# One-core transformer kernel: table loads two groups ahead, weights from block 46, 24 vector products in the first mixer, and new paces for the sparse rows

## The chip, the cores and the metric

The kernel runs as one program on one core of a Trainium2 chip. A core has five engines with an instruction queue each: TensorE (PE: matrix products; PEld is its loading of the stationary operand), VectorE (DVE), ScalarE (ACT), GpSimd (POOL) and SyncE (SP, which here issues nearly all transfers between the memory of the chip, HBM, and that of the core, SBUF). Each engine takes its instructions in order; an instruction that waits for a semaphore holds back all behind it on its engine. The metric is the device time of one execution in microseconds (us).

## The reference

The model is two blocks in a row on 512 tokens of width 1024. The first block mixes tokens (attention and a convolution), and then has a layer that picks 16 of 16,384 experts for each token and each of eight heads:

```python
def peer_ffn(h, lw):
    def chunk(xc):
        q = (xc @ wq).reshape(PEER_CHUNK, PEER_HEADS, 2, PEER_HALF)
        s = jnp.einsum('thpd,hpnd->thpn', q, keys)
        ...
        best_s, best_pos = lax.top_k(cand_s, PEER_TOPK)
        eid = jnp.take_along_axis(cand_i, best_pos, axis=-1)
        w = jax.nn.softmax(best_s.astype(jnp.float32), axis=-1).astype(xc.dtype)
        act = jax.nn.gelu(jnp.einsum('thkd,td->thk', jnp.take(u_tab, eid, axis=0), xc), approximate=False)
        return jnp.einsum('thk,thkd->td', w * act, jnp.take(v_tab, eid, axis=0))
```

Before each half of a block the activations are scaled and shifted by vectors that come from a conditioning vector: `silu(c) @ w_mod` in the first block and `silu(c_2) @ ada_w` in each layer of the second. The second block (two layers with a gated linear attention, a dense and a routed feed-forward layer) follows.

## The kernel before

**Float32 products.** TensorE multiplies in a shorter format, so each float32 operand is split into a high and a low part and each product is three matmuls (`mm3`, lines 153 to 155). `split` makes the parts of a weight tile of 128 x 1024: ScalarE copies the high part `wh` (L126), VectorE subtracts it for the low part `wl` (L128). `lin` is one product with a weight tile: 24 matmuls. `units` loads a weight tile into a buffer `raw` (L110) and splits it one ahead of its use. There are three buffers for `raw` in this part of the program, three for `wh` and three for `wl`.

**The expert layer** (`peer`) treats the tokens in two ways. For the first 384 (DN) it computes all 16,384 experts densely. For the last 128 it gathers the rows of the chosen experts.

- Dense, first table: 128 *blocks*, each one `lin` with a weight tile of `peer_u` for 384 tokens, a gelu on ScalarE (L1038), and a store of 192 KB to `Gd` in HBM (L1039).
- `choose`: top 16 of each head, and one-hot sums that turn positions into expert numbers, on VectorE, as background work that moves one step per block. `weigh` turns the choices for the dense tokens into a matrix of weights (one-hot products on VectorE, 16 small matmuls a block) and stores it to `Wd` in HBM, 2 MB for every four blocks. It begins with `turn`, which transposes the results of `choose` on TensorE (L971).
- Dense, second table: 30 *groups* (`values`) of four weight tiles of `peer_v`, 96 matmuls each, and then a 31st and 32nd. `weighted` prepares a group: it loads 768 KB of `Gd` and 768 KB of `Wd` into a buffer `gw` (L1061, L1062), multiplies them on GpSimd (L1066, four instructions), and splits the product into `cw` (L138, L139, four each).
- Sparse (`sparse`): 256 steps of one row per token each, 512 KB. GpSimd issues an indirect transfer for each row (L926), four to a buffer `rows`, one buffer ahead; VectorE multiplies a row of the first table with the tokens (L942) or adds a row of the second (L950). `pump` records so many steps per block or group.

The buffers `rows`, `gw`, `cw`, the tokens `h2h` and `h2l`, `own` and some more are *slabs*: all share one ring of 8 (`slab`).

**Vector products** (`gemv`): a modulation vector is made on VectorE, 128 elements an instruction, each with a weight tile of 512 KB (L330 loads it into a buffer `raw`, L331 multiplies and sums it). `over` spreads the conditioning vector first.

**What sets the order.** TensorE's order is that of the program. The instructions of the other engines, SP's and GpSimd's transfers among them, are put in order by a scheduler at build time, by priorities (background work has an offset: 300 for `sparse`, 100 for `choose`) and by when it reckons that they can run; buffers are given out in that order.

**Where the first mixer ends.** After attention there are three times eight products (`w_attn_o`, `w_conv_o`, `w_out`), of which 19 end with a tick of the background queues; each product uses one weight tile.

Of the kernel before, what the change touches and what calls it, by code (L numbers as in the profile page):

```python
# [11 lines left out]
F32 = mybir.dt.float32  # L12
F32R = mybir.dt.float32r
# [8 lines left out]
P = 128  # L22
# [10 lines left out]
DN = 384  # L33
# [362 lines left out]
    yield from gen  # L396


def mixer1(N):

    nc, I, sb = N.nc, N.I, N.sb
    V, A, PE, G = nc.vector, nc.scalar, nc.tensor, nc.gpsimd
    x = load_x(N)
# [9 lines left out]
    mods = sb.tile([P, 48], F32, name="mods")  # L413
# [47 lines left out]
    late = mod_multiplied(0)  # L461
# [17 lines left out]
    def gemv(f0, f1):  # L479
        return N.gemv(I["w_mod2"][f0 - 16:f1 - 16], f0, f1 - f0, lambda: cb, mods, N.v("b_mod"))  # L480
# [99 lines left out]
    for j in range(2):  # L580
        w = next(W)
# [20 lines left out]
    for h0, h1, slot in ((0, 2, 2), (2, 6, 4), (6, 8, 2)):  # L602
        ss = N.ps()
        items = []
        for h in range(h0, h1):
            pq = N.ps()
            N.lin(pq, next(W), hxh, hxl)
            i, at = slot + h - h0, 4 * (h - h0)
# [69 lines left out]
    for g in range(16):  # L678
        pg = N.ps()
        N.lin(pg, next(W), hxh, hxl)  # L680
        t = N.tmp([P, 512], name="gate")
# [39 lines left out]
    if norm:  # L721
        N.follow(delayed(delayed(norm)))
    N.lows = [V]
    N.background("gemv", gemv(24, 40), 1)
    Wa, Wc, Wo = N.units(I["w_attn_o"], 8), N.units(I["w_conv_o"], 8), N.units(I["w_out"], 8)
    ya = N.slab([P, 8, T], F32, "ya")
    for c in range(8):
# [25 lines left out]
        V.scalar_tensor_tensor(x[:, c, s], p, mods[:, 16 + c:17 + c], x[:, c, s], OP.mult, OP.add)  # L753
    last = ending(N, Wo, meh, mel, add)
    N.drain("gemv")
    return x, mods, gemv(40, 48), last


def peer(N, x, mods, last, gem=()):

    nc, I, sb = N.nc, N.I, N.sb
    V, A, PE, G = nc.vector, nc.scalar, nc.tensor, nc.gpsimd
# [238 lines left out]
    def weigh():  # L1001
# [6 lines left out]
        for q in range(DN // 8):  # L1008
# [16 lines left out]
                yield  # L1025
            o = nxt


    N.settle()
    for t in (DT, *range(DT)):  # L1030
# [3 lines left out]
    for i in range(NEXP):  # L1034
        p = N.ps()[:, :DN]
        N.lin(p, next(W), hh[:, :, :DN], hl[:, :, :DN])
        g = N.tmp([P, DN], name="gelu")
        A.activation(g, p, AF.Gelu)  # L1038
        nc.sync.dma_start(Gd[i], g)  # L1039
        if i == 9:  # L1040
            N.bg["choose"][1] = 1
            N.background("sparse", sparse(), 0, 300)
        if i == 62:
            N.drain("choose")
            N.background("pe_w", weigh(), 1)
        if i == 112:
            N.drain("pe_w")
            for e in gem:
                N.background("gemv", e, 1)
        if i > 9:  # L1050
            due += 1.2 if i < 62 else 1 if i < 112 else 1.2
            N.pump("sparse", int(due))
            due -= int(due)
    es.close()
    N.lows = [V]

    def weighted(g):

        x = N.slab([P, 2, 4, DN], F32, "gw")
        y = N.slab([P, 2, 4, DN], F32R, "cw")  # L1060
        nc.sync.dma_start(x[:, 0], Gd[4 * g:4 * g + 4].rearrange("i j t -> j i t"))  # L1061
        nc.sync.dma_start(x[:, 1].rearrange("p i t -> p (i t)"), Wd[g].rearrange("j c n -> j (c n)"))  # L1062
        w = x[:, 1].rearrange("p i t -> p (i t)").rearrange("p (c i t) -> p i c t", i=4, t=32)
        for i in range(4):
            ai = x[:, 0, i].rearrange("p (c t) -> p c t", t=32)
            G.tensor_mul(ai, ai, w[:, i])  # L1066
            N.cut(y[:, 0, i], y[:, 1, i], x[:, 0, i])
        return y

    def values(g, half, q, ps, y, s, first, last):  # L1070

# [8 lines left out]


    sums = [N.ps()[:, :DN] for _ in range(KT)]
    ahead = weighted(0)
    for g in range(30):
        y = ahead
        ahead = weighted(g + 1)
        for half in range(2):
            for _ in values(g // 2, half, g % 2, sums[4 * half:4 * half + 4], y, slice(0, DN), g == 0, g == 29):
                pass
            N.tick()  # L1090
            N.pump("sparse", 2)
    if "gemv" in N.bg:
        N.drain("gemv")
    N.drain("sparse")
    y = ahead, weighted(31)
    x = N.slab([P, KT, T], F32, "x")
    nc.sync.dma_start(x, xd)
    for k in range(KT):
# [1039 lines left out]
def build(tc, nc, I):  # L2138
    with ExitStack() as ctx:
        N = Net(ctx, tc, I)  # L2140
        N.setup()
        with tc.manual_schedule(engines={mybir.EngineType.PE}):
            with tc.tile_pool(name="early", bufs=1) as N.gp:
                N.gv = N.gp
                x, mods, late, last = mixer1(N)
                (m0, gem0), (m1, gem1) = (modulation(N, l) for l in range(2))
                x, last = peer(N, x, mods, last, (late, gem0(0, 16)))
                start = enter(N, x, last, m0)
            late = ExitStack()
            N.gp = N.late = late.enter_context(tc.tile_pool(name="late", bufs=1))  # L2150
            N.nraw = 6
            N.second()
            with tc.tile_pool(name="gemv", bufs=1) as N.gv:
                N.background("gemv", gem0(16, 48), 2)
                acc, last = mixer2(N, 0, x, *start, m0)
                start = next_input(N, x, acc, last, (0, 4, 7), N.v("ln1_g0"), N.v("ln1_b0"), m0[:, 32:40], m0[:, 24:32])
                N.background("gemv", gem1(0, 48), 1)
                x, acc, last = ffn(N, x, *start, m0)
                N.drain("gemv")
            start = next_input(N, x, acc, last, (0, 2, 3), N.v("ln2_g0"), N.v("ln2_b0"), m1[:, 8:16], m1[:, 0:8])  # L2160
            acc, last = mixer2(N, 1, x, *start, m1)
            late.close()
            N.gp = N.mp = ctx.enter_context(tc.tile_pool(name="moe", bufs=1))
            N.nraw = MOE_RAW
            moe(N, x, acc, last, m1)
# [11 lines left out]
```

## Time and profile before

| | |
|---|---|
| median of 3 runs | 3920.79 us (3920.43 to 3928.07) |
| the profiled execution | 3927.0 us, its span 3925.1 us |
| TensorE busy | 93% of the span |
| VectorE, ScalarE, GpSimd busy | 74%, 44%, 25% |
| transfers | 899 MB, 229 GB/s over the span |
| the 19 products that end the first mixer | 470.7 to 587.0 us |
| the 128 blocks, by their gelus | 769.8 to 1437.4 us |
| the 30 groups | 1444 to 2036 us |

The profile is one execution. A busy TensorE counts a matmul from its start to its modelled end, at either clock, so the granted clock has to be read beside it. The time of a stage is read from the starts of its gelus or matmuls, and what the stage waits for from the idle time of TensorE and of the engines that feed it.

### The profile page before, as it was taken

How to read it: one execution, taken by the hardware profiler on the slowest of the kernel's cores; microseconds unless marked ns; L12 is line 12 of the kernel's file. 1: busy time of each engine (PE TensorE's matmuls, PEld its weight loads, DVE VectorE, ACT ScalarE, POOL GpSimd, SP SyncE). 2: the span in 40 equal slices, each digit the busy share in tenths (PEclk: the TensorE clock that was granted, in tenths of full speed). 3: DMA queues.
4: the chain of work that ended last, by engine and by line, in shares of the span. 5: the costliest groups of instructions: out<-in, count | busy, mean ns of one | idle time of the engine just before them, and what ended most of it. 6: DMA issues, size and time to landing. Idle time of an engine off the chain costs nothing.

```text
span 3925.1 us, 61947 instructions
## 1 busy us (share of the span) xinstructions
PE 3646.8 (93%) x23129; PEld 3331.8 (85%) x23129; DVE 2897.0 (74%) x4938; ACT 1733.0 (44%) x2697; POOL 989.9 (25%) x936
## 2 busy tenths in 40 slices
PE   8999899987999778989999899999999999999996
PEld 5877778887999678889898788888889999999996
DVE  6799866999689766767855755554455788888898
ACT  3355543332444222323333223222324678787775
POOL 2212111054032344555523021002103304031211
PEclk9999999998999889999998999999998999999998
DMA  5322253389599988778864625663124799999997
GB/s 217 98 68 97 95 198 111 102 313 340 179 320 334 360 310 297 288 289 295 303 232 147 193 96 168 188 198 102 60 94 184 262 335 331 339 341 339 338 349 256
DMA packets 314758, 898.97 MB, mean 229 GB/s; under 512 B 28179, under 2 KB 114451, under 8 KB 312783
## 3 DMA queue, kind: packets, MB, share of 16 engines
q1 hardware_dynamic: 273583, 747.68, 55.7%
q0 software_dynamic: 40864, 147.25, 9.9%
q8 instruction: 183, 3.00, 0.3%
q14 instruction: 128, 1.05, 0.1%
HBM read 816.35 MB, written 78.46 MB: 228 GB/s over the span
## 4 chain that ended last, share of the span: by engine, by line
PE 39%; DMA 9%; DVE 6%; issue 5%; POOL 3%; ACT 2%; SPq 0%; DVEq 0%; POOLq 0%; ACTq 0%
PE ps L1819 10%; PE ps L154 9%; PE ps L155 9%; PE ps L153 9%; DMA gw<-Wd 3%; DVE wl L128 2%; DMA raw<-in_peer_v_dram 2%; ACT wh L126 1%; DMA rows<-in_peer_urows_dram,own 1%; DMA raw<-in_ada_w_dram 1%; DVE cw L139 1%; POOL gw L1066 1%; DMA rows<-in_peer_vrows_dram,own 1%; POOL mod L312 1%; DVE raw L331 1%
## 5 line engine op out<-in xcount | busy, mean ns | idle before, releaser
L126 ACT ACTIVATE wh<-raw 128x1024 fp32r<-128x1024 f32 (+1 forms) x1014 | 1050.2, 1042 | 1131.1 <-PE ps L154 594.9
L128 DVE TENSOR_TENSOR wl<-raw,wh 128x1024 fp32r<-128x1024 f32 (+1 forms) x1000 | 1221.5, 1235 | 310.9 <-ACT wh L126 295.0
L155 PE MATMUL ps<-h2h,wl 128*128 128x384 f32 (+2 forms) x1176 | 413.6, 352 | 46.1 <-DVE wl L128 46.1
L153 PE MATMUL ps<-h2h,wh 128*128 128x384 f32 (+2 forms) x1176 | 420.8, 358 | 32.1 <-ACT wh L126 27.7
L155 PE MATMUL ps<-cw,wl 128*128 128x384 f32 (+2 forms) x1088 | 376.0, 346 | 47.2 <-DVE wl L128 47.1
L154 PE MATMUL ps<-h2l,wh 128*128 128x384 f32 (+2 forms) x1176 | 410.2, 349 | 2.3 <-DVE h2l L139 2.1
L153 PE MATMUL ps<-cw,wh 128*128 128x384 f32 (+2 forms) x1088 | 372.5, 342 | 15.9 <-ACT wh L126 15.9
L154 PE MATMUL ps<-cw,wh 128*128 128x384 f32 (+2 forms) x1088 | 371.3, 341 | 0.0
L155 PEld LDWEIGHTS ps<-h2h,wl 128*128 128x128 f32 x1176 | 229.0, 195 | 59.9 <-DVE wl L128 55.1
L154 PE MATMUL ps<-ul,wh 128*128 128x512 f32 (+1 forms) x712 | 269.7, 379 | 8.5 <-DVE ul L139 7.8
L926 POOL DMA_INDIRECT rows<-in_peer_urows_dram,own x128 | 183.6, 1435 | 368.9 <-issue 203.4
L153 PE MATMUL ps<-uh,wh 128*128 128x512 f32 (+1 forms) x712 | 272.6, 383 | 3.4 <-ACT uh L138 2.3
L155 PE MATMUL ps<-uh,wl 128*128 128x512 f32 (+1 forms) x712 | 267.3, 375 | 0.0
L155 PEld LDWEIGHTS ps<-cw,wl 128*128 128x128 f32 x1088 | 215.7, 198 | 58.1 <-DVE wl L128 58.0
L153 PEld LDWEIGHTS ps<-h2h,wh 128*128 128x128 f32 x1176 | 229.6, 195 | 40.2 <-ACT wh L126 30.9
L331 DVE SCALAR_TENSOR_TENSOR raw<-raw,over 128x1024 f32<-128x1024 f32 x128 | 158.5, 1245 | 129.5 <-DMA raw<-in_ada_w_dram 105.3
L154 PEld LDWEIGHTS ps<-h2l,wh 128*128 128x128 f32 x1176 | 229.4, 195 | 7.8 <-DVE h2l L139 3.7
L926 POOL DMA_INDIRECT rows<-in_peer_vrows_dram,own x128 | 165.0, 1289 | 277.0 <-PE ps L971 88.1
L153 PEld LDWEIGHTS ps<-cw,wh 128*128 128x128 f32 x1088 | 215.7, 198 | 18.7 <-ACT wh L126 18.7
L950 DVE SCALAR_TENSOR_TENSOR own<-rows,own 128x1024 f32<-128x1024 f32 x127 | 171.0, 1346 | 74.3 <-DMA rows<-in_peer_vrows_dram,own 73.8
L942 DVE SCALAR_TENSOR_TENSOR rows<-rows,own 128x1024 f32<-128x1024 f32 x128 | 175.2, 1378 | 66.7 <-DMA rows<-in_peer_urows_dram,own 53.1
L1819 PE MATMUL ps<-xe,wh 128*128 128x352 f32 (+3 forms) x1408 | 221.9, 309 | 1.5 <-DVE xe L139 1.5
(529 smaller groups left out, 8579.7 us busy)
## 6 DMA issues: line engine op xcount, KB each, us to landing
raw<-in_moe_gu_dram SPq DMA_DIRECT2D x352, 512.0 KB, 5.8
raw<-in_moe_down_dram SPq DMA_DIRECT2D x160, 512.0 KB, 5.6
raw<-in_peer_v_dram SPq DMA_DIRECT2D x136, 512.0 KB, 6.2
raw<-in_peer_u_dram SPq DMA_DIRECT2D x128, 512.0 KB, 6.5
raw<-in_ada_w_dram SPq DMA_DIRECT2D x96, 512.0 KB, 4.4
raw<-in_w_in_dram SPq DMA_DIRECT2D x88, 512.0 KB, 3.9
Gd<-gelu SPq DMA_DIRECT2D x128, 192.0 KB, 5.4
Wd<-wst SPq DMA_DIRECT2D x12, 2048.0 KB, 14.1
```

The source lines that it names most:

```text
L126: self.nc.scalar.activation(h, src, AF.Copy)
L128: self.lows[-1].tensor_sub(l, src, f32(h))
L139: self.nc.vector.tensor_sub(l, src, f32(h))
L153: mm(out, ah, bh, start=start, stop=False)
L154: mm(out, ah, bl, start=False, stop=False)
L155: mm(out, al, bh, start=False, stop=stop)
L312: self.nc.gpsimd.tensor_scalar(t, x[:, k], sc[:, k:k + 1], sh[:, k:k + 1], OP.mult, OP.add)
L331: V.scalar_tensor_tensor(r, r, 1.0, b, OP.mult, OP.mult, accum_out=out[:, f:f + 1])
L926: G.indirect_dma_start(out=g[:, j], out_offset=None, in_=I[table], in_offset=bass.IndirectOffsetOnAxis(ap=oid[:, a:a + 1], axis=0))
L942: V.scalar_tensor_tensor(g[:, j], g[:, j], 1.0, ox, OP.mult, OP.mult, accum_out=oact[:, a:a + 1])
L950: V.scalar_tensor_tensor(oy, g[:, j], oact[:, a:a + 1], oy, OP.mult, OP.add)
L1819: PE.matmul(ps[j % 2][:, 0:n * (2 - i)], w[i][:, j * P:(j + 1) * P], rs[j // 2][i], start=first and i == 0 and j < 2, stop=last and i == p ...
```

## The change

- `weighted` is parted in two: `weights(g)` issues the two loads of group g, `weighted(x)` multiplies and splits. The loads of groups 0 and 1 are recorded at block 118, group 0 is made at block 125, and in the loop the loads run two groups ahead (before: one call made loads and products of the next group).
- `weigh` begins after block 46 (before 62), and what is left of `choose` is recorded at once there; `weigh` is drained at block 94 (before 112).
- Of the sparse rows 0.6 are recorded per block up to block 45, 1 up to 93, 1.6 up to 127 (before: 1.2 up to 61, 1 up to 111, 1.2 up to 127). Two per half group follow as before.
- The last 8 vector products of the first block's modulation and the first 16 of the second's (`gem0(0, 16)`), which were recorded from block 112 on, are recorded in the end of the first mixer, at two per tick; the 16 that were there already also go at two per tick.

```diff
@@ -396,7 +396,7 @@
     yield from gen
 
 
-def mixer1(N):
+def mixer1(N, gem):
 
     nc, I, sb = N.nc, N.I, N.sb
     V, A, PE, G = nc.vector, nc.scalar, nc.tensor, nc.gpsimd
@@ -721,7 +721,9 @@
     if norm:
         N.follow(delayed(delayed(norm)))
     N.lows = [V]
-    N.background("gemv", gemv(24, 40), 1)
+    N.background("gemv", gemv(24, 48), 2)
+    for e in gem:
+        N.background("gemv", e, 2)
     Wa, Wc, Wo = N.units(I["w_attn_o"], 8), N.units(I["w_conv_o"], 8), N.units(I["w_out"], 8)
     ya = N.slab([P, 8, T], F32, "ya")
     for c in range(8):
@@ -753,10 +755,10 @@
         V.scalar_tensor_tensor(x[:, c, s], p, mods[:, 16 + c:17 + c], x[:, c, s], OP.mult, OP.add)
     last = ending(N, Wo, meh, mel, add)
     N.drain("gemv")
-    return x, mods, gemv(40, 48), last
-
-
-def peer(N, x, mods, last, gem=()):
+    return x, mods, last
+
+
+def peer(N, x, mods, last):
 
     nc, I, sb = N.nc, N.I, N.sb
     V, A, PE, G = nc.vector, nc.scalar, nc.tensor, nc.gpsimd
@@ -1025,6 +1027,24 @@
                 yield
             o = nxt
 
+    def weights(g):
+
+        x = N.slab([P, 2, 4, DN], F32, "gw")
+        nc.sync.dma_start(x[:, 0], Gd[4 * g:4 * g + 4].rearrange("i j t -> j i t"))
+        nc.sync.dma_start(x[:, 1].rearrange("p i t -> p (i t)"), Wd[g].rearrange("j c n -> j (c n)"))
+        return x
+
+    def weighted(x):
+
+        y = N.slab([P, 2, 4, DN], F32R, "cw")
+        w = x[:, 1].rearrange("p i t -> p (i t)").rearrange("p (c i t) -> p i c t", i=4, t=32)
+        for i in range(4):
+            ai = x[:, 0, i].rearrange("p (c t) -> p c t", t=32)
+            G.tensor_mul(ai, ai, w[:, i])
+            N.cut(y[:, 0, i], y[:, 1, i], x[:, 0, i])
+        return y
+    loads = []
+
 
     N.settle()
     for t in (DT, *range(DT)):
@@ -1040,32 +1060,21 @@
         if i == 9:
             N.bg["choose"][1] = 1
             N.background("sparse", sparse(), 0, 300)
-        if i == 62:
+        if i == 46:
             N.drain("choose")
             N.background("pe_w", weigh(), 1)
-        if i == 112:
+        if i == 94:
             N.drain("pe_w")
-            for e in gem:
-                N.background("gemv", e, 1)
+        if i == 118:
+            loads += [weights(0), weights(1)]
+        if i == 125:
+            ahead = weighted(loads.pop(0))
         if i > 9:
-            due += 1.2 if i < 62 else 1 if i < 112 else 1.2
+            due += 0.6 if i < 46 else 1 if i < 94 else 1.6
             N.pump("sparse", int(due))
             due -= int(due)
     es.close()
     N.lows = [V]
-
-    def weighted(g):
-
-        x = N.slab([P, 2, 4, DN], F32, "gw")
-        y = N.slab([P, 2, 4, DN], F32R, "cw")
-        nc.sync.dma_start(x[:, 0], Gd[4 * g:4 * g + 4].rearrange("i j t -> j i t"))
-        nc.sync.dma_start(x[:, 1].rearrange("p i t -> p (i t)"), Wd[g].rearrange("j c n -> j (c n)"))
-        w = x[:, 1].rearrange("p i t -> p (i t)").rearrange("p (c i t) -> p i c t", i=4, t=32)
-        for i in range(4):
-            ai = x[:, 0, i].rearrange("p (c t) -> p c t", t=32)
-            G.tensor_mul(ai, ai, w[:, i])
-            N.cut(y[:, 0, i], y[:, 1, i], x[:, 0, i])
-        return y
 
     def values(g, half, q, ps, y, s, first, last):
 
@@ -1080,19 +1089,17 @@
 
 
     sums = [N.ps()[:, :DN] for _ in range(KT)]
-    ahead = weighted(0)
     for g in range(30):
         y = ahead
-        ahead = weighted(g + 1)
+        loads.append(weights(g + 2))
+        ahead = weighted(loads.pop(0))
         for half in range(2):
             for _ in values(g // 2, half, g % 2, sums[4 * half:4 * half + 4], y, slice(0, DN), g == 0, g == 29):
                 pass
             N.tick()
             N.pump("sparse", 2)
-    if "gemv" in N.bg:
-        N.drain("gemv")
     N.drain("sparse")
-    y = ahead, weighted(31)
+    y = ahead, weighted(loads.pop(0))
     x = N.slab([P, KT, T], F32, "x")
     nc.sync.dma_start(x, xd)
     for k in range(KT):
@@ -2142,9 +2149,9 @@
         with tc.manual_schedule(engines={mybir.EngineType.PE}):
             with tc.tile_pool(name="early", bufs=1) as N.gp:
                 N.gv = N.gp
-                x, mods, late, last = mixer1(N)
                 (m0, gem0), (m1, gem1) = (modulation(N, l) for l in range(2))
-                x, last = peer(N, x, mods, last, (late, gem0(0, 16)))
+                x, mods, last = mixer1(N, (gem0(0, 16),))
+                x, last = peer(N, x, mods, last)
                 start = enter(N, x, last, m0)
             late = ExitStack()
             N.gp = N.late = late.enter_context(tc.tile_pool(name="late", bufs=1))
```

**SP in the end of the first mixer** (L110 loads a weight tile of `w_conv_o`, L330 that of a vector product, both into one of the three `raw` buffers; the `sg` are gates). Before:

```order
L110 DMA raw_4377<-in_w_conv_o_dram 128x1024
L330 DMA raw_4407<-in_w_mod_dram 128x1024
L743 DMA sg_4497<-gates 128x512
L110 DMA raw_4418<-in_w_conv_o_dram 128x1024
L330 DMA raw_4448<-in_w_mod_dram 128x1024
L110 DMA raw_4460<-in_w_conv_o_dram 128x1024
```

After, at the same place:

```order
L110 DMA raw_4369<-in_w_conv_o_dram 128x1024
L745 DMA sg_4556<-gates 128x512
L330 DMA raw_4399<-in_w_mod_dram 128x1024
L330 DMA raw_4402<-in_w_mod_dram 128x1024
L110 DMA raw_4414<-in_w_conv_o_dram 128x1024
L330 DMA raw_4444<-in_w_mod_dram 128x1024
L330 DMA raw_4447<-in_w_mod_dram 128x1024
```

Per product the queue now holds three loads for the three buffers, where it held two.

**VectorE where `weigh` begins** (`wl` is the low part of a block's weights, L881/L883 the sums of `choose` into `pk`, L994 to L1000 the first one-hots of `weigh`). Before, the low parts of the 59th to the 66th block:

```order
L128 TENSOR_TENSOR wl_8729<-raw_8726,wh_8728 128x1024
L901 TENSOR_REDUCE z_8756<-pk_6184 128x8
L902 RECIPROCAL z_8756<-z_8756 128x8
L903 TENSOR_TENSOR pk_6184<-pk_6184,z_8756 128x128
L128 TENSOR_TENSOR wl_8770<-raw_8767,wh_8769 128x1024
...
L128 TENSOR_TENSOR wl_9018<-raw_9015,wh_9017 128x1024
L998 TENSOR_TENSOR oh_9004<-iota,wij_8971 128x1024
```

After, the low parts of the 50th and the 51st block and the 33 instructions between them, of which eight stand here:

```order
L128 TENSOR_TENSOR wl_8464<-raw_8461,wh_8463 128x1024
...
L888 TENSOR_TENSOR oh_8366<-kk_8125,steps 128x1024
L889 TENSOR_TENSOR oh_8367<-oh_8366,kk_8125 128x1024
L883 TENSOR_REDUCE pk_6275<-oh_8367 128x64
...
L981 TENSOR_TENSOR wij_8417<-ws_8422,wij_8417 128x768
...
L1000 TENSOR_TENSOR oh_8450<-iota,wij_8417 128x1024
...
L899 TENSOR_TENSOR oh_8378<-oh_8377,kk_8125 128x1024
L883 TENSOR_REDUCE pk_6275<-oh_8378 128x64
L996 TENSOR_TENSOR oh_8451<-iota,wij_8417 128x1024
...
L128 TENSOR_TENSOR wl_8528<-raw_8525,wh_8527 128x1024
```

Before, `choose` was through by the 59th low part, with seven low parts between it and the first one-hot of `weigh`. After, the last part of the choices stands right before `weigh`, in one piece. On TensorE `turn` stands in the middle of a block in both (after: of block 47, whose low part is the 48th).

**SP and VectorE among the groups.** SP, before and after, at the same group:

```order
L110 DMA raw_14014<-in_peer_v_dram 128x1024
L110 DMA raw_14044<-in_peer_v_dram 128x1024
L1061 DMA gw_14435<-Gd 128x4x384
L1062 DMA gw_14435<-Wd 128x1536
L110 DMA raw_14076<-in_peer_v_dram 128x1024
```

```order
L1033 DMA gw_14274<-Gd 128x4x384
L1034 DMA gw_14274<-Wd 128x1536
L110 DMA raw_14028<-in_peer_v_dram 128x1024
L110 DMA raw_14065<-in_peer_v_dram 128x1024
```

VectorE before, where `gw_14435` is cut:

```order
L128 TENSOR_TENSOR wl_14047<-raw_14044,wh_14046 128x1024
L139 TENSOR_TENSOR cw_14436<-gw_14435,cw_14436 128x384
L128 TENSOR_TENSOR wl_14079<-raw_14076,wh_14078 128x1024
L950 SCALAR_TENSOR_TENSOR own_6223<-rows_14428,own_6223 128x1024
L139 TENSOR_TENSOR cw_14436<-gw_14435,cw_14436 128x384 x3
```

and after, where `gw_14274` is cut:

```order
L128 TENSOR_TENSOR wl_14176<-raw_14173,wh_14175 128x1024
L952 SCALAR_TENSOR_TENSOR own_6314<-rows_14351,own_6314 128x1024
L139 TENSOR_TENSOR cw_14422<-gw_14274,cw_14422 128x384 x4
L128 TENSOR_TENSOR wl_14215<-raw_14212,wh_14214 128x1024
L952 SCALAR_TENSOR_TENSOR own_6314<-rows_14351,own_6314 128x1024
```

Before, the first cut of a group stood behind the low part of the weight tile whose load was issued just ahead of the group's own loads (`raw_14044`). After, four weight tiles and the loads of another group lie between: `raw_14173` is the fifth tile behind `gw_14274`.

## Rows read from the trace of the kernel before

**Rows 1.** The page's first part: span, then busy time, share, instructions.

```profile
span 3925.1 us, 61947 instructions
...
PE 3646.8 (93%) x23129; PEld 3331.8 (85%) x23129; DVE 2897.0 (74%) x4938; ACT 1733.0 (44%) x2697; POOL 989.9 (25%) x936
```

**Rows 2.** Busy time of engines by stretch, then granted clock, DMA share, GB/s.

```profile
470.70:587.00 116.30, 111.38 (x474) 88.10 (x473) 77.00 (x141) 54.34 (x73) 14.56 (x20) 0.99 0.54 179
862.00:963.00 101.00, 78.00 (x397) 74.03 (x396) 100.40 (x201) 28.63 (x43) 57.33 (x43) 0.90 0.93 358
1064.00:1316.00 252.00, 251.94 (x1933) 236.37 (x1930) 221.41 (x309) 117.57 (x194) 72.81 (x47) 1.00 0.99 322
1300.00:1350.00 50.00, 31.88 (x187) 29.42 (x185) 34.70 (x44) 9.85 (x18) 19.80 (x16) 0.83 1.05 386
1316.00:1444.00 128.00, 82.58 (x375) 76.64 (x375) 93.06 (x121) 34.39 (x61) 55.54 (x46) 0.81 0.95 344
1444.00:2036.00 592.00, 535.54 (x2880) 522.03 (x2881) 401.68 (x435) 177.14 (x243) 284.40 (x216) 0.95 0.79 288
2003.00:2036.00 33.00, 33.00 (x192) 33.00 (x191) 14.61 (x17) 8.39 (x8) 0.00 (x0) 1.00 0.60 208
```

**Rows 3.** Starts of the gelus, two stretches: times ns, first and last start us.

```profile
L1038 ACT ACTIVATE gelu<-ps x25: 469/490/492, 862.0 to 995.8; 128x384 f32<-128x384 f32 x25
...
L1038 ACT ACTIVATE gelu<-ps x14: 469/470/494, 995.8 to 1050.9; 128x384 f32<-128x384 f32 x14
```

**Rows 4.** Who waited for whom from 1444 to 2036 us: total us, times, longest.

```profile
POOL gw L1066 <- DMA gw<-Wd: 126.9, 17, 13.6
...
DVE own L950 <- DMA rows<-in_peer_vrows_dram,own: 70.6, 24, 6.8
...
DVE rows L942 <- DMA rows<-in_peer_urows_dram,own: 51.4, 22, 9.5
PE ps L155 <- DVE wl L128: 47.1, 30, 6.5
...
PE ps L153 <- ACT wh L126: 15.9, 9, 6.6
```

**Rows 5.** The costliest groups of instructions: busy us, mean ns, idle before.

```profile
L128 DVE TENSOR_TENSOR wl<-raw,wh 128x1024 fp32r<-128x1024 f32 (+1 forms) x1000 | 1221.5, 1235 | 310.9 <-ACT wh L126 295.0 <-PE ps L796 4.9
...
L126 ACT ACTIVATE wh<-raw 128x1024 fp32r<-128x1024 f32 (+1 forms) x1014 | 1050.2, 1042 | 1131.1 <-PE ps L154 594.9 <-issue 143.5 <-PE ps L155 98.5
...
L926 POOL DMA_INDIRECT rows<-in_peer_urows_dram,own x128 | 183.6, 1435 | 368.9 <-issue 203.4 <-DVE own L950 66.4 <-ACT wst L1022 31.3
L942 DVE SCALAR_TENSOR_TENSOR rows<-rows,own 128x1024 f32<-128x1024 f32 x128 | 175.2, 1378 | 66.7 <-DMA rows<-in_peer_urows_dram,own 53.1 <-issue 13.5
L950 DVE SCALAR_TENSOR_TENSOR own<-rows,own 128x1024 f32<-128x1024 f32 x127 | 171.0, 1346 | 74.3 <-DMA rows<-in_peer_vrows_dram,own 73.8
L1066 POOL TENSOR_TENSOR gw<-gw 128x384 f32<-128x384 f32 x128 | 167.7, 1342 | 196.9 <-DMA gw<-Wd 176.7 <-DMA raw<-in_w_mod_dram 8.6 <-PE ps L155 6.2
...
L331 DVE SCALAR_TENSOR_TENSOR raw<-raw,over 128x1024 f32<-128x1024 f32 x128 | 158.5, 1245 | 129.5 <-DMA raw<-in_ada_w_dram 105.3 <-DMA raw<-in_w_mod_dram 23.8
```

**Rows 6.** Transfers of the whole run: KB each, median us from issue to landing.

```profile
raw<-in_peer_v_dram SPq DMA_DIRECT2D x136, 512.0 KB, 6.2
...
gw<-Wd SPq DMA_DIRECT2D x32, 768.0 KB, 7.9
...
rows<-in_peer_urows_dram,own POOLq DMA_INDIRECT x128, 8.8
```

**Rows 7.** Loads into the `raw` buffers, issued from 483 to 558 us.

```profile
DMA to landing us min/median/max: 3.5/4.7/8.2
```

**Rows 8.** VectorE's groups of instructions from 770 to 963 us.

```profile
L881 DVE TENSOR_REDUCE pk<-oh 128x64 f32<-128x1024 f16 x18 | 21.6, 1212 | 0.0
...
L886 DVE TENSOR_TENSOR oh<-kk,steps 128x1024 f16<-128x1024 f16 x6 | 3.8, 681 | 0.0
```

**Rows 9.** SP's queue after the last store to `Wd`: start, us.

```profile
1322.50 20.31 SPq L330 DMA_DIRECT2D raw<-in_w_mod_dram  x1
```

## The prediction

> **What bounds the kernel now.** I read the first part of the page, then busy time by stretch. TensorE is busy for 93% of the span [rows 1], so a gain can only come from stretches in which it waits or runs at the lower clock. Rows 2 show three. From 862 to 963 us VectorE is busy 100.4 of 101 us and TensorE 78: VectorE bounds these blocks. From 1316 to 1444 us, the last 16 blocks, TensorE is busy 82.6 of 128 us at a granted clock of 0.81, and the DMA engines 0.95 of the time at 344 GB/s. From 1444 to 2036 us, the 30 groups, it takes 592 us, where the last two groups take 33.0 (192 matmuls without a gap at clock 1.00): 16.5 us a group, 495 for 30. So 97 us are lost there. From 1064 to 1316 us, by contrast, TensorE has no gap.
>
> What the groups lose their time to is in the waits [rows 4]: TensorE waits 47.1 us for low parts of weights and 15.9 for high parts, and the clock of 0.95 costs 5% of 535, some 27; together 90 of the 97. VectorE, which makes the low parts in order, stands 70.6 and 51.4 us for gathered rows, and GpSimd 126.9 us for `gw`. Why these go together: GpSimd issues the gathers and multiplies `gw` in one queue. While it waits for `gw` (7.9 us from issue to landing, rows 6), the next gathers are not issued; the rows come late; a low part stands behind a row on VectorE; TensorE waits for it. The order adds that the loads of `gw` stood one weight tile ahead of the cuts that need them.
>
> **The change part by part.** All terms are against the profiled execution, 3927.0 us (span 3925.1 and 1.9 around it).
>
> *The end of the first mixer: +20.* 24 vector products more: 24 x 1.245 = 30 us of VectorE [rows 5], which is busy 77 of 116.3 us there [rows 2], so its time alone is hidden. The buffers are not. Each product now needs three loads, and there are three. A buffer of a vector product is taken for landing 4.7 [rows 7], the product 1.3 and SP's issue 0.35: 6.4 us; that of a weight tile for 4.7, 1.04, 1.24 [rows 5] and 0.35: 7.3. The mean is 6.7 us a product, where the 19 took 116.3 / 19 = 6.1: +11. But 24 x 0.52 = 12.6 MB more raise 179 GB/s to some 287, at which the loads of the groups land after 6.2 [rows 2, 6]: then 8.2 us a product, +39. Three loads in flight hold 1.57 MB, which at 287 GB/s is 5.5 us; that gives 7.5 and +26. I take +20. Ends: 0 (landing 3.5 throughout, rows 7) and +45.
>
> *Blocks 24 to 48: -32.* 25 gelus lie 133.8 us apart, where 14 later ones lie 55.1 apart, 4.24 a block [rows 3]; at that pace 24 blocks take 101.8. The scheduler put 54 rows between these blocks' low parts before and 14 after: 40 x 1.36 = 54 us less for VectorE [rows 5], more than the 32 that it is late. Ends: -33 and -20.
>
> *The start of `weigh`: +23.* Here a new wait is added. `turn` stands in the middle of block 47 on TensorE and needs all choices. The low part of the 50th block can be made only when block 46 has given its buffer back, and the last choices stand behind it on VectorE. Up to the last sum they are 6 reductions of 1.212, 12 one-hot steps of 0.68 [rows 8], one step of 0.95, some 2 of small ones, and the low part of 1.24: 19.7 us, of which half a block (2.1) covers TensorE. 18 us are waited, and all later matmuls stand behind that. In the stretch with the long gaps the clock was 0.81 [rows 2]; 25 us at that clock lose 5. Ends: +10 and +30. Before, seven low parts lay between.
>
> *The other blocks: -2.* `weigh` takes 252 us as before; TensorE fills them [rows 2]. Blocks 48 to 63.5, which took 68 us at the pace of rows 3, and the 128 us of the last 16 blocks go; 32 blocks without `weigh` come. They carry 64 rows (33.5 MB), 32 weight tiles (16.8), 32 gelu stores (6.3), five groups' `gw` (7.9) and the last `Wd` (2.1): 66.6 MB. At the 344 GB/s of the last blocks before that is 194 us; TensorE needs 32 x 4.24 = 136. VectorE has 32 x 1.24 + 64 x 1.36 = 127. So the transfers bound it: 194 - 196 = -2. The scheduler put 56 of the 64 rows into the first 16 of these blocks, so little of it hides behind the rest. What went well before may go badly here too: behind the last store to `Wd` a load stood 20.3 us in SP's queue [rows 9]. Ends: -24 (172 us at 386 GB/s, the fastest of rows 2, which lasted 50 us) and +35 (231 us at 288).
>
> A page weighs on this term. HBM Reference of the Trainium skill (Specifications) has it that a core that streams alone, its neighbour idle, measures about 425 GB/s, and about 358 beside a streaming neighbour. No stretch here shows more than 386, and that for 50 us [rows 2]. By 425 the 66.6 MB would take an estimated 157 us and the term would be -39; by the row it is -2, and the row is taken.
>
> *The 30 groups: -69.* The loads of `gw` now stand five weight tiles ahead of the first cut, some 20 us, against 7.9 to land [rows 6] and 1.3 for the first product [rows 5]. So GpSimd no longer waits, and the gathers are issued as soon as their slab is free. What is late next: the weight tiles' own landing. I leave the 15.9 us behind high parts, a quarter of the 47.1, and no more than that of the clock: 495 + 28 = 523. The transfers allow it: 25 groups' `gw` (39 MB), 120 tiles (63) and 116 rows (61) are 163 MB, 312 GB/s over 523 us. Ends: -92 (500 us) and -26 (163 MB at 288 GB/s: 566).
>
> *After the groups: +3.* Ten rows more stand in the last two groups, 13 us on VectorE, which is busy 14.6 of 33 there [rows 2]; hidden but for a wait for a gather. Ends 0 and +13.
>
> Sum: 20 - 32 + 23 - 2 - 69 + 3 = -57. 3927 - 57 = 3870; the profiled execution is 6.2 above the median of the runs, so 3864.
>
> **The rivals.**
>
> *The transfers give no more than they gave the groups: slower.* If the 288 GB/s of the groups [rows 2] are what the DMA engines reach with gathers among the loads, and no result of late issue, the 32 blocks take 231 (+35) and the groups 566 (-26): 20 - 32 + 23 + 35 - 26 + 3 = +23, 3944. It decides below 297 GB/s, where 229.6 MB take the 774 us that would balance the sum. For it: a DMA share of 0.79 over the whole stretch. Against: 344 GB/s with the same mix just before.
>
> *Gathers stay the bound.* In the built program `gw` and `rows` share three slabs after the change, with one set of gathers in flight. A set takes four issues of 1.4, landing 8.8 and one row of 1.35: 15.8, and if GpSimd waits some 2.6 for the cut that frees the slab, 18.4 a group: 552 us, -40. The sum is then -28: 3893. For it: the waits for rows in rows 4. Against: the gathers alone are under 16.5.
>
> *All goes well.* Groups at 500, the 32 blocks at 172, the first mixer hidden: -32 + 23 - 24 - 92 + 3 = -122, 3799. Against: the DMA share of 0.95 in the last blocks [rows 2].
>
> *The first mixer eats it: no change.* With the slowest landing of rows 7, 8.2, a product takes 10.2 us: +78 in place of +20, sum +1, 3922. Against: it is the slowest, not the median.
>
> **How the numbers follow.** Forecast 47%, gathers 22%, all well 12%, transfers 12%, first mixer 7%. What is within 0.2% (8 us) can't be told from no change. Faster: nearly all of the forecast and of the gathers and the whole of the good case, 0.80. Same: most of the first mixer and a little of the gathers, 0.07. Slower: the transfers and one in a hundred of the rest, 0.13. The range takes in the good case at one end, 3800, and ends between no change and the transfers' rival at 3925; outside are most of the latter and half of the good case, under 2 in 10.
>
> **What would show it.** First mixer: the 19 products over some 136 us, with VectorE waiting for loads of L331's tiles. Blocks 24 to 48 at 4.24 us a gelu. A gap of TensorE of 18 us in block 47, released by VectorE's L883. The 32 blocks after `weigh` at some 6 us with 0.95 DMA share. The groups at 17.4 us, GpSimd's wait for `gw` near none, VectorE's for rows less than half. The prediction is wrong if the groups stay above 18.5 us, if the first mixer loses over 45 us, or if the gap in block 47 isn't there.

## Result and the profile after

The changed kernel takes 3954.86 us (median of 4 runs, 3952.0 to 3962.27), the kernel before on the same chip 3923.74: a ratio of 1.0083, 95% interval 1.0068 to 1.0098. It is slower by 31 us, where 57 us less were forecast. The profiled execution has a span of 3950.2 us, 25.1 more than before.

The page's first part of the kernel after; TensorE has the same work as in [rows 1].

```profile
span 3950.2 us, 61941 instructions
...
PE 3646.1 (92%) x23129; PEld 3328.6 (84%) x23129; DVE 2904.9 (74%) x4938; ACT 1735.7 (44%) x2697; POOL 1003.1 (25%) x936
```

Busy time by stretch of the kernel after: start:end, length, then the engines, granted clock, DMA share, GB/s. The stretches are the 19 products that end the first mixer (bounded as in [rows 2], where they took 116.3 us: from the first matmul to the issue of the last tile's load), blocks 24 to 46, `weigh`, the 32 blocks after it, the 30 groups.

```profile
478.20:615.60 137.40, 122.38 (x519) 95.12 (x518) 101.56 (x189) 56.32 (x77) 20.38 (x21) 0.96 0.68 228
890.00:986.00 96.00, 93.04 (x519) 92.72 (x518) 65.53 (x176) 35.12 (x48) 7.33 (x6) 0.98 0.63 222
1012.00:1264.00 252.00, 252.00 (x1917) 237.09 (x1915) 220.47 (x308) 119.68 (x196) 73.41 (x48) 1.00 0.97 322
1264.00:1472.00 208.00, 152.75 (x760) 145.26 (x758) 127.58 (x147) 52.82 (x86) 85.11 (x73) 0.87 0.82 303
1472.00:2064.00 592.00, 530.90 (x2879) 518.20 (x2879) 408.73 (x432) 178.31 (x251) 314.94 (x228) 0.96 0.78 289
```

The row to look at is the last: the groups, in which 69 us were to be won, take 592 us as in [rows 2], at the same rate, 289 GB/s for 288. VectorE's load from block 24 on, by contrast, fell as forecast (66 of 96 us busy, where it was 100 of 101).

Starts of the gelus after, two stretches (times in ns, first and last start in us):

```profile
L1058 ACT ACTIVATE gelu<-ps x23: 472/473/493, 887.7 to 986.4; 128x384 f32<-128x384 f32 x23
...
L1058 ACT ACTIVATE gelu<-ps x12: 472/472/491, 1011.5 to 1068.0; 128x384 f32<-128x384 f32 x12
```

The 23 lie 4.5 us apart, against 5.6 in the first row of [rows 3]. Between the two rows is the gap that `turn` makes: 25.1 us, for 4.2 at TensorE's pace. What TensorE waited for from 986 to 1012 us (total us, times, longest):

```profile
PE ps L973 <- DVE pk L883: 13.1, 2, 10.2
PE ps L973 <- DVE pk L905: 2.7, 1, 2.7
```

Who waited for whom in the groups after, from 1472 to 2064 us:

```profile
ACT wh L126 <- DMA raw<-in_peer_v_dram: 205.4, 51, 12.1
POOL gw L1043 <- DMA gw<-Wd: 111.1, 19, 10.4
DVE own L952 <- DMA rows<-in_peer_vrows_dram,own: 75.9, 32, 9.6
DVE rows L944 <- DMA rows<-in_peer_urows_dram,own: 74.9, 29, 7.9
...
POOL rows L928 <- DVE cw L139: 65.3, 17, 10.1
PE ps L155 <- DVE wl L128: 57.0, 32, 8.2
```

Two of these waits in the kernel before, from 1444 to 2036 us:

```profile
ACT wh L126 <- DMA raw<-in_peer_v_dram: 86.0, 30, 8.9
...
POOL rows L926 <- DVE cw L139: 44.7, 9, 7.8
```

GpSimd still waits 111 us for `gw` (126.9 in [rows 4]), VectorE more than before for rows (151 us for 122), TensorE 57.0 us for low parts (47.1). ScalarE waits 205 us for weight tiles (86.0 before). And GpSimd has a second wait in the same queue: before it can issue gathers it waits for a cut on VectorE, which frees the slab, 65.3 us for 44.7. The transfers of that stretch, median us to landing last (a tile took 6.7 in the groups before):

```profile
raw<-in_peer_v_dram SPq DMA_DIRECT2D x120, 512.0 KB, 9.3
...
gw<-Wd SPq DMA_DIRECT2D x27, 768.0 KB, 9.8
...
rows<-in_peer_urows_dram,own POOLq DMA_INDIRECT x56, 9.9
```

Why GpSimd still waits is in the chain of waits of the kernel after (start us, us, what):

```profile
1673.89 9.99 DMA gw<-Wd
...
1685.14 4.58 POOL gw L1043 x3
...
1690.87 1.72 POOL rows L928
...
1695.18 9.86 DMA rows<-in_peer_urows_dram,own
```

The load that is recorded two groups ahead is followed at once by its own multiplication, and the next gathers stand behind that. Pairing SP's `Wd` loads with the first multiplication and the last cut of the same group (groups 4 to 29, medians), the load is issued 9.3 us ahead of the multiplication before and 10.0 after; from there to the end of the cut it is 9.3 before and 27.9 after; and the finished product then lies 60 us before and 50 after until TensorE takes it. So the lead that was won lies behind the multiplication, where no one needs it.

### The profile page after: what moved, and what is told of

Same layout as the page of the kernel before. It is cut to its first block, busy times and chain, and to the rows that moved or that the text cites. A ratio compares the mean times of both kernels' runs of the same rounds, so it can differ in the third digit from the quotient of the medians.

```text
span 3950.2 us, 61941 instructions
## 1 busy us (share of the span) xinstructions
PE 3646.1 (92%) x23129; PEld 3328.6 (84%) x23129; DVE 2904.9 (74%) x4938; ACT 1735.7 (44%) x2697; POOL 1003.1 (25%) x936
## 4 chain that ended last, share of the span: by engine, by line
PE 43%; DMA 9%; DVE 6%; POOL 4%; issue 4%; ACT 1%; SPq 0%; DVEq 0%; POOLq 0%; ACTq 0%
PE ps L155 10%; PE ps L154 10%; PE ps L153 10%; PE ps L1826 10%; DMA rows<-in_peer_urows_dram,own 2%; DMA gw<-Wd 2%; DVE wl L128 2%; DMA rows<-in_peer_vrows_dram,own 1%; DMA raw<-in_peer_v_dram 1%; POOL gw L1043 1%; ACT wh L126 1%; POOL rows L928 1%; DVE rows L944 1%; DVE cw L139 1%; DMA raw<-in_moe_gu_dram 1%
## 5 line engine op out<-in xcount | busy, mean ns | idle before, releaser
L331 DVE SCALAR_TENSOR_TENSOR raw<-raw,over 128x1024 f32<-128x1024 f32 x128 | 156.5, 1230 | 93.7 <-DMA raw<-in_ada_w_dram 84.4
```

Of the source, the lines that this page charges most:

```text
L331: V.scalar_tensor_tensor(r, r, 1.0, b, OP.mult, OP.mult, accum_out=out[:, f:f + 1])
```

## The experiments

Theories for the groups. **Q**, the queue: the scheduler put the multiplication right behind its load, on GpSimd's one queue; gathers, rows, low parts follow late. **S**: the slabs that `gw` and rows share. **R**: the three buffers for weight tiles. **G**: one set of gathers in flight. **D**: the transfers give no more than 289 GB/s (the prediction's first rival). Ratios are to the kernel before on the same chip, with 95% intervals; "groups" is from the first matmul of group 0 to the last of group 29.

**e1_cw2.** Two fixed slabs for `cw`.

```diff
+        if len(cws) < 2:
+            cws.append(N.slab([P, 2, 4, DN], F32R, "cw"))
+        else:
+            cws.append(cws.pop(0))
+        y = cws[-1]
```

> The changed kernel, with the split products `cw` in two fixed slabs by turns, so that `gw` and `rows` share five slabs where the changed kernel left them three. The 30 groups took 592 us in the changed kernel, and 592 before. Theory S (the slabs: loads of `gw` and gathers wait for each other's buffers): the groups fall to 520 to 550 us, the kernel to 3885 to 3915, and GpSimd's wait for `gw` (111 us) goes below 40. Theory D (289 GB/s is what the transfers give with gathers among them): groups 585 to 600, kernel within 10 us of 3955. Theory R (three buffers for weight tiles, each held for its landing): groups 580 to 600 as well, and ScalarE's wait for tiles of `peer_v` (205 us) stays.

Measured: 3958.0 us, ratio 1.0078 (1.0057 to 1.0100); groups 597; GpSimd's wait for `gw` 120 us. S falls in this form: the room that came free only let GpSimd multiply earlier still (load to multiplication 9.0 us, multiplication to cut 69). The gathers' wait for a cut stayed, 66.6 us, so e1 doesn't say what that wait costs.

**e2_raw7.** Four more buffers, in turns with the three, during the groups.

```diff
+        if self.more:
+            self.turns += 1
+            if self.turns % 7 % 2 == 0:
+                return self.more.tile([P, 1024], F32, name=self.name("raw"), tag="rawx", bufs=4)
```

> The changed kernel, with seven buffers for the weight tiles of the 30 groups in place of three (in the room that the one-hot tiles leave). Theory R (the tile's landing, 9.3 us, in three buffers): groups at 530 to 560 us instead of 592, kernel 3890 to 3925, ScalarE's wait for tiles (205 us) below 60. Theory S (slabs): groups 580 to 595, since GpSimd's chain is not touched. Theory D (the transfers' rate): groups 585 to 600, landing of a tile longer than 9.3 us, rate still 285 to 293 GB/s.

Measured: 3924.5 us, 0.9991 (0.9981 to 1.0000); groups 565.5, at 298 GB/s. That lies just above the range of R (530 to 560) and below those of S and D: R is part of it (27 us), D is shaken.

**e3_cw2_raw7.** Both edits.

> Both edits at once: `cw` in two fixed slabs and seven buffers for weight tiles in the groups. Theory D: groups 580 to 600 us still, at 285 to 293 GB/s. Theories S and R: the groups at 500 to 530 us, 320 GB/s or more, kernel 3865 to 3895; if only one of the two is the bound, as that one alone.

Measured: 3924.7 us, 0.9986 (0.9973 to 0.9998); groups 562.4, as e2 alone. But the stretch has two parts (columns as above):

```profile
1468.00:1847.00 379.00, 335.00 (x1823) 327.39 (x1822) 257.17 (x268) 116.18 (x161) 203.36 (x148) 0.95 0.79 283
1847.00:2030.00 183.00, 183.00 (x1058) 183.00 (x1057) 162.25 (x163) 67.99 (x93) 98.76 (x80) 1.00 0.90 335
```

GpSimd's two waits in the second part:

```profile
POOL rows L933 <- DVE cw L144: 57.0, 9, 8.9
...
POOL gw L1052 <- DMA gw<-Wd: 2.6, 1, 2.6
```

The first 19 groups take 20.0 us each, the last 11 take 16.6, with all their loads and gathers, at 335 GB/s. That contradicts D. In these last groups the load lies 11 to 24 us (median 18) ahead of its multiplication, and of GpSimd's 80 us of waits for `gw` 2.6 fall here: this led to Q. The gathers' wait for a cut is long here, 57.0 us, and TensorE loses nothing by it (busy all of the 183 us).

**e4_half.** Gathered rows half as long in the groups.

```diff
-                G.indirect_dma_start(out=g[:, j], out_offset=None, in_=I[table],
+                G.indirect_dma_start(out=g[:, j, :512] if n >= 16 else g[:, j], out_offset=None,
+                                     in_=I[table].rearrange("n (b c) -> (n b) c", b=2) if n >= 16 else I[table],
```

> The changed kernel, with each gathered row half as long in the groups (2 KB in place of 4 KB for each of 128 tokens; half of each such row is left out of the result); the instructions, their order and their buffers stay. About 31 of the 171 MB of the groups go. Theory D (bytes at 289 GB/s): 140 MB take 484 us, so the groups come near TensorE's floor, 500 to 515 us instead of 592, and the kernel to 3870 to 3885. Theories S and R (chains of waits): the landings get shorter by a few us but the chains stay, groups 550 to 590, kernel 3915 to 3955.

Measured: 3895.8 us (one run); groups 535.8, at 261 GB/s, GpSimd's wait for `gw` 112 us. Between the two expectations: less to move shortens every landing (a gathered row 6.7 us for 9.9), but the rate falls well under 289, so it isn't a fixed rate that binds; it doesn't tell Q from R.

**e5_late.** The multiplication for group g+1 also waits for the first half of group g-1.

```diff
-            G.tensor_mul(ai, ai, w[:, i])
+            m = G.tensor_mul(ai, ai, w[:, i])
+            if mark:
+                N.tc.add_manual_dep(m.ins if hasattr(m, "ins") else m, mark, mybir.DependencyInfo(
+                    mybir.DependencyClass.Sync, mybir.DependencyReason.DATA), reason="late")
```

> The changed kernel, in which GpSimd's multiplication for group g+1 also waits for the first half of group g-1 on TensorE, so that it can't be put right behind its load. In the changed kernel 10.0 us (median) lie between the issue of a group's `Wd` load and its multiplication, 9.3 before, and the split products lie ready 50 us before their use. Theory Q (the lead of the loads was given away: the multiplication was moved up right behind the load, GpSimd stands for it and the gathers behind it): the distance rises above 18 us, GpSimd's wait for `gw` (111 us) falls below 30, the groups go from 592 to 525 to 560 us, the kernel to 3890 to 3925. Theory G (one set of gathers in flight, about 10 us of landing): the wait for `gw` goes, VectorE's waits for rows (151 us) stay above 120, groups 580 to 600, kernel 3940 to 3965. Theory R (three buffers for weight tiles, already shown to be worth 27 us of groups) as theory G.

Measured: 3924.7 us, 0.9992 (0.9980 to 1.0003); groups 555.9; load to multiplication 29.3 us. The waits of its groups:

```profile
POOL gw L1043 <- PE ps L153: 269.5, 29, 91.3
...
ACT wh L126 <- DMA raw<-in_peer_v_dram: 131.7, 33, 11.1
...
DVE own L952 <- DMA rows<-in_peer_vrows_dram,own: 50.1, 27, 5.2
DVE rows L944 <- DMA rows<-in_peer_urows_dram,own: 49.3, 28, 5.4
...
PE ps L155 <- DVE wl L128: 27.5, 18, 3.4
```

GpSimd waits for no `gw` load any more, and though it now waits much longer, for TensorE, rows come earlier (99 us of waits for 151) and TensorE's wait for low parts halves. The groups fit Q; the whole is at the edge of its range. The gathers still stand right behind the multiplication, but they no longer wait for a cut either (65.3 us without this edit, none here): the later multiplication takes away two waits at once, and the scheduler placed other work anew around it, so e5 shows what the edit is worth and not which wait made it so.

**e6_rows3.** Fixed slabs (made as in e1): three for rows with two sets in flight, two each for `gw` and `cw`.

```diff
+            while len(ahead) < (1 if N.fix is None else 2) and (job := next(more, None)):
+                ahead.append(gather(*job))
```

> The changed kernel, with fixed slabs in the groups: three for gathered rows and two sets of gathers in flight, two for `gw`, two for `cw`. Theory G: VectorE's waits for rows (151 us) fall below 60 and the groups to 530 to 560 us, kernel 3890 to 3925. Theory Q: GpSimd still stands over 80 us for `gw`, but that no longer reaches VectorE: also faster, groups 550 to 575. Theory R: rows' waits fall, TensorE then waits for weight tiles, groups 575 to 595, kernel 3935 to 3960.

Measured: 3959.4 us, 1.0074 (1.0057 to 1.0091); groups 606. All expectations of a gain miss: the scheduler issued all gathers in groups 0 to 8 (groups 3 to 8 took 32 us each), and left the rest without any. The first row below is groups 2 to 8, the second the others behind them.

```profile
1492.00:1709.00 217.00, 147.21 (x673) 138.13 (x672) 201.53 (x230) 43.09 (x69) 165.04 (x128) 0.82 0.98 377
1709.00:2065.00 356.00, 356.00 (x2017) 356.00 (x2016) 169.60 (x174) 129.56 (x169) 108.84 (x80) 1.00 0.63 210
```

It says little on G, but shows 377 GB/s over 217 us with gathers.

**e7_rows3_raw7.** e6 with the buffers of e2.

> The same fixed slabs with two sets of gathers in flight, and seven buffers for weight tiles in the groups. If late rows and the three buffers together are what holds the groups (G and R): 500 to 520 us, the pace at which twelve groups ran when both the slabs and the buffers were widened (16.7 us), kernel 3860 to 3885. If GpSimd's wait for `gw` is a bound of its own (Q): 550 to 570, as with seven buffers alone.

Measured: 3909.5 us, 0.9948 (0.9928 to 0.9967); groups 543.6. Between the two, and not to be read as either: the last gather is issued in group 15, so the last 12 groups, at 16.6 us, have no row left to gather, and the first 18, at 19, carry all of them. It says as little on G as e6.

**e8_late_raw7.** e5 and e2 together.

> The later multiplication and seven buffers for weight tiles. Q and R together: groups 505 to 530 us, kernel 3870 to 3895. R alone: 560 to 570 us, kernel 3920 to 3930. G: not below 560.

Measured: 3882.0 us, 0.9888 (0.9871 to 0.9904); groups 505.4. The groups, and two waits in them:

```profile
1453.00:1959.00 506.00, 502.35 (x2883) 500.93 (x2881) 403.06 (x430) 187.21 (x257) 348.25 (x241) 1.00 0.90 331
```

```profile
POOL gw L1048 <- PE ps L158: 172.1, 22, 85.3
...
PE ps L160 <- DVE wl L133: 3.6, 3, 2.8
```

TensorE is busy 502 of 506 us, with one set of gathers in flight as before, so G falls, and at 331 GB/s, so D falls. With e2 and e5 this is a full square of the two edits: 592, 566, 556, 505. Alone they bring 27 and 36, together 87: each alone leaves the other's wait in place.

**e9_before_late_raw7.** The same two edits in the kernel before.

> The kernel before, with the two edits that brought the changed kernel's groups to 505 us: the multiplication waits for the first half of group g-1 on TensorE, and seven buffers for weight tiles. The loads stay recorded one group ahead. Theory Q (the scheduler gave away the lead, however far ahead the load is recorded): the distance from load to multiplication goes from 9.3 to over 18 us here too, the groups from 592 to 510 to 540 us (eight vector products lie in them), and the kernel to 3845 to 3880. If the recording of loads two groups ahead is needed as well: the distance stays below 14 us, groups above 555, kernel above 3890.

Measured: 3848.5 us, 0.9798 (0.9776 to 0.9820); groups 502.9, at 344 GB/s, a little better than expected. The load is recorded one group ahead here and needs no more: two groups ahead bring nothing of their own. The distance was expected above 18 us and is 12.5, and GpSimd still waits 66 us for `gw`; but VectorE's waits for rows of the first table are down to 4.8 us. So neither the distance nor the wait for `gw` alone decides: the gathers still stand behind the multiplication here. What is gone is their wait for a cut, of which this run shows none:

```profile
POOL gw L1073 <- DMA gw<-Wd: 66.2, 9, 11.5
...
DVE rows L947 <- DMA rows<-in_peer_urows_dram,own: 4.8, 2, 3.1
```

With seven buffers either wait alone was borne (this one here, that for a cut in the last groups of e3), and both together were not (e2: 82 and 90 us); the kernel before and the changed one have both, 172 and 176 us together. Beside e8, whose edits are the same, the kernel stands 0.9% lower: the rest of the change costs some 35 us.

**e10_before_early7.** e9 with the four buffers from block 112.

> The same, with the four more buffers for weight tiles opened at block 112 already, where the one-hot tiles are last used. If the three buffers also held the last 16 blocks (128 us in the kernel before, with TensorE busy 82.6): those blocks at 95 to 115 us, kernel 15 to 30 us below the run before. If the transfers' rate holds them (0.95 of the DMA engines' time): no change, within 8 us.

Measured: 3841.1 us, 0.9774 (0.9748 to 0.9800). The last 16 blocks (from the gelu of block 111 to the first group) go from 113.7 to 100.6 us as expected, the kernel only 7 us, less than expected and inside the intervals; in the profiled execution the blocks began 6.2 us later than in e9 (first gelu 773.8 and 767.6 us), in a part that the edit doesn't touch. These blocks:

```profile
1322.00:1421.70 99.70, 70.37 (x372) 67.45 (x371) 76.25 (x101) 28.19 (x45) 33.40 (x25) 0.86 1.00 384
```

**e11_all.** e8, with the buffers also in the first mixer's end and after `weigh`, and `weigh` at block 57.

```diff
-        if i == 46:
+        if i == 57:
...
+    N.more = N.room.enter_context(N.phase("rawm"))
     meh, mel = N.slab([P, 8, T], F32R, "meh"), N.slab([P, 8, T], F32R, "mel")
```

> The changed kernel with the later multiplication, four more buffers for weight tiles from the end of `weigh` on and in the last 16 products of the first mixer, and `weigh` begun at block 57, when `choose` has run out by itself, instead of 46 (rows 0.8 a block up to there). Expected against the run with late multiplication and seven buffers (3882): the gap of 25 us at block 47 goes (-15 to -21), the 26 us lost at the end of the first mixer shrink by 5 to 20 if the buffers made them and not the transfers, the blocks after `weigh` gain 0 to 25: 3825 to 3860. If the gap and the mixer's loss are made by the transfers, 3870 to 3885.

Measured: 3830.2 us, 0.9747 (0.9729 to 0.9765). At the start of `weigh` TensorE waits 2.0 us in all; the first gelu starts at 783.0 us (781.8 in e12). In the nine profiles with the changed kernel's first mixer it starts at 788.3 to 796.2, in the three with that of before at 767.6 to 773.8, so the four buffers, the only edit that lies ahead of it, took away about half of the first mixer's loss. The blocks after `weigh`:

```profile
1281.00:1403.00 122.00, 104.83 (x592) 102.09 (x590) 88.04 (x99) 40.37 (x64) 59.63 (x44) 0.93 1.00 383
```

**e12_rows.** e11 with 15 more rows in the groups.

```diff
-            N.pump("sparse", 2)
+            N.pump("sparse", 2 if half or g < 15 else 3)
```

> The run with all edits together (3830 us), with three rows instead of two in the first half of each of the first 15 groups, so that no rows are left behind the last group. In that run 12 row instructions of 1.2 to 1.3 us stood on VectorE between the last group and the sums that free TensorE, which waited 22.5 us there. If those rows make that wait: 10 to 20 us less, 3810 to 3820. If the fifteen rows cost the groups as much (17.0 us a group now), 3825 to 3835.

Measured: 3827.5 us, 0.9733 (0.9717 to 0.9749). By a slip the third row went to the second fifteen groups, not the first. The wait that it was to take away went from 22.5 us to

```profile
PE ps L158 <- DVE x L1125: 4.6, 1, 4.6
```

but the groups begin 7 us later, and the whole is not to be told from e11. Both are 2.5 to 2.7% below the kernel before and, by the ratios, 3.3 to 3.5% below the changed one.

## Why the prediction was wrong

Five of its six terms came out within 11 us, one failed, and that one carried the forecast. All from the two profiled executions; each measured term is the change of the lag from one row to the next:

| term | forecast | measured | read from |
|---|---|---|---|
| end of the first mixer | +20 | +26.2 | first gelu 769.8, 796.0 |
| blocks 24 to 48 (measured to 46) | -32 | -27.1 | gelu of block 46: 987.3, 986.4 |
| start of `weigh` | +23 | +20.5 | gelu of block 48: 995.8, 1015.4 |
| other blocks | -2 | +8.7 | first group: 1443.9, 1472.2 |
| 30 groups | -69 | +0.2 | their end: 2035.9, 2064.4 |
| after the groups | +3 | -3.4 | span: 3925.1, 3950.2 |
| sum | -57 | +25.1 | |

A term is good to a few us only: in nine profiles with the same first mixer the first gelu started between 788.3 and 796.2 us.

**The step that failed** is "The loads of `gw` now stand five weight tiles ahead of the first cut, some 20 us ... So GpSimd no longer waits, and the gathers are issued as soon as their slab is free." The lead was read up to the cut, on ScalarE and VectorE. But GpSimd waits with the multiplication, and that one the scheduler had moved up to its load: 10.0 us behind it, of which 9.8 are landing. The trace of before already held the sign: its products lay finished 60 us ahead of their use, so `gw` was not late for TensorE at all. It was in the way of the gathers, and an earlier load doesn't cure that as long as the multiplication is moved up with it. And "as soon as their slab is free" was not soon: the gathers waited 65.3 us for the cut that frees it, now 27.9 us behind the multiplication. e5 and e8 show it from the other side: a *later* multiplication, which makes GpSimd wait longer in all (for TensorE), is worth 36 us alone and 60 with the buffers.

**What else was missed in that term**: "What is late next: the weight tiles' own landing" was right, but priced at 15.9 + a quarter of 47.1. In the changed kernel ScalarE waits 205 us for tiles (86 before), which land after 9.3 us (6.7); the buffers are worth 27 us alone (e2) and 50 after the first edit (e5 to e8). The floor of 16.5 us a group was right: 16.6 in most groups of e8.

**The terms that came out.** The end of the first mixer was near in size: the 19 products took 137.4 us (some 136 forecast), and 7.5 us more came in ahead of them. That is partly luck: the three buffers, from which the term was worked out, made about half of the loss (e11), and it is not VectorE that waits for the tiles of L331 (7.3 us, 16.3 before), as forecast, but ScalarE for the products' own tiles (33.0 us). At the start of `weigh` the mechanism was right: TensorE waits 15.8 us for the choices (18 forecast), 13.1 of them behind L883, and the granted clock from 986 to 1012 us averaged 0.67.

**The rivals.** "The transfers give no more" forecast 3944, nearest to the 3955 measured, and by the wrong cause: the groups run at 331 GB/s (e8) and 344 (e9) with the same mix, so 288 was what late issue left. "Gathers stay the bound" came closest in kind, though it forecast a gain: it named the right queue, and its wait of 2.6 us a group for the cut that frees the slab was 2.2. It left out the 3.7 us a group for `gw`, and five slabs in place of three bring nothing (e1), since the scheduler spent them on multiplying earlier still. The prediction's own signs were sound: groups above 18.5 us (19.7 measured) are what it said would prove it wrong, and the wait for `gw` that should be near none is 111 us.

**The transfers.** The term "other blocks" went by 344 GB/s; they ran at 303, hence +9, inside its range. With more buffers such blocks reach 383 and 384 GB/s (e10, e11). HBM Reference of the Trainium skill (Specifications) has about 425 for a core that streams alone; the most that a run here shows is 405 over 100 us (e7, 1523 to 1623 us) and 413 over 50 (e11, 1325 to 1375 us), so the page's figure is not reached, but 344 was not the limit either. Nor was the 386 that the prediction took as the fastest: the trace of before itself has 411 from 863 to 913 us.

What stays open: which of GpSimd's two waits, for `gw` and for the cut, made the gathers late (no run with three buffers has one without the other and is otherwise alike), whether one of the two edits would do in the kernel before (only both together were run), and what makes the first mixer's remaining 12 us or so.

## What to carry to other kernels

Before loading earlier to remove a wait, find out on which queue the waiting instruction stands, what is behind it, and how long its result lies before it is used. If the result lies long (60 us here), the instruction is not late but may be in the way: tie it to its consumer, so that a scheduler which believes in quick landings can't move it up to its load. And judge buffers by landing time: a stretch at 0.78 of the DMA engines with an engine waiting for loads may want more buffers, not fewer bytes.

## What the hardware showed

- Loads and gathers together ran at 383 and 384 GB/s at a DMA share of 1.00 over 122 and 100 us (e11, e10), with TensorE at work; with three buffers the same kind of blocks showed 303 to 344. The fastest 100 us of any run are at 405 GB/s (e7, in groups with some seven gathers each instead of four).
- In e12 groups 0 to 18 take 16.64 us each, and groups 20 to 24 take 16.96, as do all in e11; TensorE has no gap in either, and the granted clock reads 1.00 in both. Why was not tried.
